# Second-layer scan of a two-layer hybrid trunk: TensorE's order fixed to the program's, with the fp32 matmuls and transposes of a chunk in one block

## The chip, the core and the metric

The kernel runs on one core of one Trainium2 chip. The metric is the device time of one execution in microseconds, the median of several runs. A profile of one execution shows where its time goes; the engines are named as on its page: PE is TensorE (matmuls and transposes), PEld its weight loads, DVE VectorE, ACT ScalarE, POOL GpSimd, SP the queue from which all transfers are issued.

## What is computed

Two layers over 1024 tokens of width 1024: a gated DeltaNet layer and a Mamba-2 layer, each with a residual add, then a final RMSNorm. The change concerns the second layer alone:

```python
proj = hid @ w_in                                   # 1024 x 6176
z, xbc, dt = split(proj)                            # 2048, 4096, 32
xbc = silu(causal_conv(xbc, conv_w) + conv_b)
xs, Bm, Cm = split(xbc)                             # 32 heads x 64; 8 groups x 128, twice
# chunks of 128 tokens, 8 groups of 4 heads
cb     = C_chunk @ B_chunk.T                        # per group
y_diag = (cb * exp(acs_l - acs_s), lower) @ X       # per head
states = B.T @ (decay * X);  S = S * dec + states   # per group, chunk after chunk
y_off  = C @ S_before * exp(acs)
y = rmsnorm_per_group((y_diag + y_off + D * xs) * silu(z))
out = x + y @ w_out
```

## The kernel before

**Tiling.** Tokens stand in eight chunks of 128. The normalised input of a layer is kept transposed as `hid`, split into a high and a low part, and every projection is three matmuls of parts (L165 to L167, L227 to L229), so that the product has nearly fp32 precision. The scan's own products are plain fp32 matmuls, and 128 x 128 transposes are matmuls against an identity (L66).

**Second layer.** A loop over the eight head groups (L949 to L959; it starts at -1 to produce the first group's inputs) runs two generators side by side for eight slots. `J` makes the next group's inputs: each slot is one projection half, 24 matmuls of 512 columns into one bank `ps_proj` (`proj_halves`), whose result is copied, convolved by three operations on DVE (L204) and passed through SiLU. For the half of the channels that are X, four transposes (`ps_pt<-ident,acc`) are put into a list, `later`, and are issued behind the next half's matmuls or by `flush()`. `S` is the scan of the present group (`scan`), one chunk per slot:

- `store(n-1)` transposes the normalised result `yn` of the chunk before (two L66 transposes into `ps_tr`), scales it and sends it to DRAM for the output projection;
- `prep(n+1)` makes B·C for the next chunk (L856) and B transposed (L66, `ps_tr<-ident,BC`), the decay matrix `lt` by four exponentials on ACT (L866) from the rows `gcrow`, and their product `mt` on DVE (L868). The rows come by four transfers for every four chunks (L316) and are masked by four operations on POOL (L317);
- `z_chunk` is the gate z for the chunk: 24 matmuls of 256 columns into `ps_proj`;
- `main(n)` is the state update (L882), C·S (L892) and the diagonal products: 16 matmuls of 64 columns (L895, L896), each into one half of the partitions. Their sum goes through five operations on DVE, a square with a sum on ACT (L906), two small operations on POOL (L907, L909) and a scaling on DVE (L910), which gives `yn`.

The last group has no J; it computes two z chunks per slot in its first four slots, and the output projection (L347 to L349) follows.

**What sets the order.** The kernel is written in this program order, but the order in which an engine gets its instructions is chosen by the scheduler, from the dependencies, the program's order as priority and a model of the engines' times. Each engine then takes its instructions in the order given.

Of the kernel before, what the change touches and what calls it, by code (L numbers as in the profile page):

```python
# [1 line left out]

# [17 lines left out]
NT = T // P  # L20
# [4 lines left out]
def hybrid_trunk(  # L25
# [194 lines left out]
    def z_chunk(pool, hid, zw, n, z=None):  # L220
        zh, zl = zw
        pt = ps_proj()[:, 0:256]
        th, o = n // 4, (n % 4) * P
        for k in range(KT):
            xh = hid["h", k // 4, th][:, k % 4, o:o + P]
            xl = hid["l", k // 4, th][:, k % 4, o:o + P]
            nc.tensor.matmul(pt, xh, zh[:, k, :], start=k == 0, stop=False)  # L227
            nc.tensor.matmul(pt, xh, zl[:, k, :], start=False, stop=False)  # L228
            nc.tensor.matmul(pt, xl, zh[:, k, :], start=False, stop=k == KT - 1)  # L229
        tz = pool.tile([P, 256], F32, tag="tz", name="tz", bufs=1)  # L230
        if z is None:
            z = pool.tile([P, 256], F32, tag="z", name="z", bufs=2)
        nc.scalar.activation(tz, pt, AF.Tanh, scale=0.5)
        nc.vector.scalar_tensor_tensor(out=z, in0=tz, scalar=1.0, in1=pt, op0=ALU.add, op1=ALU.mult)  # L234
        return z
# [167 lines left out]
    with tc.tile_pool(name="gw", bufs=2) as gw:  # L403
# [360 lines left out]
        for g in range(8):  # L764
            J = todo["K"] if g == 0 else js_of(g)
# [37 lines left out]
    with tc.tile_pool(name="sw", bufs=2) as sw:  # L803
# [39 lines left out]
        def scan(g):  # L843
# [5 lines left out]
            def prep(n):  # L849
                if n % 4 == 0:  # L850
                    for h in range(4):
                        rows[h] = gc_rows(sw, "gcrow", Gs["gcr"], h0 + h, n // 4, 4)
                c = slice(n * P, (n + 1) * P)
                BT, CT, xn_ = BC[:, 0, c], BC[:, 1, c], xs[:, n, :]
                pt = ps_tr()
                nc.tensor.matmul(pt[:, 0:P], BT, CT, start=True, stop=True)  # L856
                btok = xw = None
                if n < NT - 1:
                    turn_pe(pt[:, P:2 * P], BT, ident)
                    xw = sw.tile([P, 256], F32, tag="xw", name="xw")  # L860
                    nc.gpsimd.tensor_tensor(out=v4(xw), in0=v4(xn_), in1=bc4(dtd, n), op=ALU.mult)
                    btok = sw.tile([P, P], F32, tag="bt", name="bt")
                    nc.scalar.activation(btok, pt[:, P:2 * P], AF.Copy, scale=0.5)
                lt = sw.tile([P, 4, P], F32, tag="L", name="lt")
                for h in range(4):
                    nc.scalar.activation(lt[:, h, :], rows[h][:, n % 4, :], AF.Exp, bias=ldt[:, h0 + h, n:n + 1])  # L866
                mts = sw.tile([P, 4, P], F32, tag="M", name="mt")
                nc.vector.tensor_tensor(out=mts, in0=pt[:, 0:P].unsqueeze(1).broadcast_to([P, 4, P]), in1=lt,  # L868
                                        op=ALU.mult)
                t2 = sw.tile([P, 256], F32, tag="t2", name="t2")  # L870
                nc.gpsimd.tensor_tensor(out=v4(t2), in0=v4(xn_),
                                        in1=dskip[:, h0:h0 + 4].unsqueeze(2).broadcast_to([P, 4, 64]), op=ALU.mult)
                A[n] = btok, xw, mts, t2
# [40 lines left out]
            def store(n):  # L914
                yn = Y.pop(n)
                pt = ps_tr()
                yg = sw.tile([P, 2, P], F32, tag="yg", name="yg")
                for i in range(2):
                    turn_pe(pt[:, i * P:(i + 1) * P], yn[:, i * P:(i + 1) * P], ident)
                for i in range(2):  # L920
                    nc.scalar.activation(yg[:, i, :], pt[:, i * P:(i + 1) * P], AF.Copy,
                                         scale=snw[:, 2 * g + i:2 * g + i + 1])
                nc.sync.dma_start(yd1[n][g * 256:(g + 1) * 256, :].rearrange("(h p) t -> p h t", p=P), yg)
# [4 lines left out]
            if g == 7:  # L928
                zt = bpool.tile([P, NT, 256], F32, tag="a0", name="z7", bufs=2)
            for n in range(NT):  # L930
                if n > 0:
                    store(n - 1)
                if n < NT - 1:
                    prep(n + 1)
                if g < 7:
                    Z[n] = z_chunk(sw, hid2, zw, n)
                elif n < 4:
                    for m in (2 * n, 2 * n + 1):
                        Z[m] = z_chunk(sw, hid2, zw, m, zt[:, m, :])
                S = main(n, S, Z.pop(n))  # L940
                yield
            store(NT - 1)

# [5 lines left out]
        for g in range(-1, 8):  # L949
            its = [bc_halves(g + 1) if g >= 0 else bc0, x_halves(g + 1)] if g < 7 else []  # L950
            J = (y_ for it in its for y_ in it)
            S = scan(g) if g >= 0 else iter(())
            for slot in range(8):
                next(S, None)
                next(J, None)
            flush()
            next(S, None)
            if g < 7:
                GS[g + 1]["zw"] = load_zw(bpool, sw_in, (g + 1) * 256, ("a2", "a3"), 2)  # L959

# [33 lines left out]
```

## Time and profile before

| | us |
|---|---|
| median of 3 runs | 1995.43 (1994.64 to 2000.03) |
| the profiled execution's own time | 1990.66 |
| its span on the chip | 1989.0 |
| PE busy | 1919.1 (96%) |
| DVE busy | 1305.7 (66%) |
| ACT busy | 1063.4 (53%) |
| POOL busy | 411.6 (21%) |

The span runs from the first to the last instruction; 1.66 us of the execution's time lie around it. Busy PE is not PE at its peak: matmuls overlap, so the time that one costs is the distance from its start to the start of the next. In a timeline row, x2 joins two neighbouring instructions (each fp32 product of L856, L882 and L892 shows as two), and a bracket at its end names an idle stretch before the row and what ended it.

### The profile page before, as it was taken

The page shows a single profiled execution, that of the slowest core. Times are in us where ns is not written, and L with a number is a line of the kernel's source. Part 1 is how long each engine was busy: PE and PEld are TensorE (multiplying, and loading weights), DVE is VectorE, ACT ScalarE, POOL GpSimd, SP SyncE. Part 2 cuts the span into 40 slices and gives each one's busy share as a digit, 9 for nine tenths or more (in the row PEclk, how much of TensorE's full clock was granted, in tenths as well). Part 3 has the DMA queues.
Part 4 walks back from the last instruction along what each step waited for, and adds up shares of the span by engine and source line. Part 5 has one row for each costly group of instructions (what it writes and reads, how often), then busy time and mean ns, then how long its engine had stood idle before and what let it go on. Part 6 is the DMA issues. An engine that isn't in the chain of part 4 may idle for free.

```text
span 1989.0 us, 36043 instructions
## 1 busy us (share of the span) xinstructions
PE 1919.1 (96%) x12974; PEld 1639.7 (82%) x12974; DVE 1305.7 (66%) x2915; ACT 1063.4 (53%) x2893; POOL 411.6 (21%) x818
## 2 busy tenths in 40 slices
PE   7997999999999999999999999999999999999998
PEld 5786888888888888897778788888888888888886
DVE  6797685778677776844354676657666676767333
ACT  5635656575656666564343554544555555555332
POOL 1101211212122212100000032423333243332000
PEclk9997999999999999999999999999999999999999
DMA  4421323232232323235574232222222223236654
GB/s 141 117 54 49 98 56 84 67 78 75 57 93 52 99 49 105 58 94 157 152 221 133 64 91 80 69 84 80 64 80 57 80 75 83 78 104 195 203 170 142
DMA packets 284789, 193.35 MB, mean 97 GB/s; under 512 B 65425, under 2 KB 246338, under 8 KB 284610
## 3 DMA queue, kind: packets, MB, share of 16 engines
q1 hardware_dynamic: 284610, 191.05, 34.2%
q8 instruction: 102, 1.67, 0.4%
q14 instruction: 77, 0.63, 0.1%
HBM read 159.34 MB, written 31.65 MB: 96 GB/s over the span
## 4 chain that ended last, share of the span: by engine, by line
PE 75%; DMA 9%; DVE 7%; ACT 4%; POOL 2%; issue 2%; SPq 1%; POOLq 0%; DVEq 0%; ACTq 0%
PE ps_proj L165 9%; PE ps_proj L166 9%; PE ps_proj L167 9%; PE ps_proj L347 6%; PE ps_proj L349 6%; PE ps_proj L348 5%; PE ps_proj L227 5%; PE ps_proj L228 4%; PE ps_proj L229 4%; DMA gcrow<-gcr_s 2%; PE ps_tr L66 2%; PE ps_pt L66 2%; DMA X<-xd 2%; DVE acc L204 2%; PE ps_sc L895 1%
## 5 line engine op out<-in xcount | busy, mean ns | idle before, releaser
L165 PE MATMUL ps_proj<-hid_h,wh 128*128 128x512 f32 x1024 | 412.9, 403 | 3.4 <-ACT acc L200 3.2
L167 PE MATMUL ps_proj<-hid_h,wl 128*128 128x512 f32 x1024 | 404.9, 395 | 0.0
L166 PE MATMUL ps_proj<-hid_l,wh 128*128 128x512 f32 x1024 | 403.6, 394 | 0.0
L227 PE MATMUL ps_proj<-zh,hid_h 128*128 128x256 f32 x1024 | 300.5, 293 | 1.0 <-DVE z L234 1.0
L229 PE MATMUL ps_proj<-zh,hid_l 128*128 128x256 f32 x1024 | 295.4, 288 | 0.0
L228 PE MATMUL ps_proj<-zl,hid_h 128*128 128x256 f32 x1024 | 295.4, 288 | 0.0
L165 PEld LDWEIGHTS ps_proj<-hid_h,wh 128*128 128x128 f32 x1024 | 192.7, 188 | 43.9 <-ACT acc L200 4.0
L167 PEld LDWEIGHTS ps_proj<-hid_h,wl 128*128 128x128 f32 x1024 | 192.5, 188 | 40.3
L166 PEld LDWEIGHTS ps_proj<-hid_l,wh 128*128 128x128 f32 x1024 | 192.9, 188 | 35.4
L347 PE MATMUL ps_proj<-woh,yh 128*128 128x512 f32 x512 | 205.2, 402 | 4.6 <-ACT yh L86 3.2
L348 PE MATMUL ps_proj<-wol,yh 128*128 128x512 f32 x512 | 204.4, 400 | 0.8 <-DVE wol L87 0.7
L349 PE MATMUL ps_proj<-woh,yl 128*128 128x512 f32 x512 | 203.1, 399 | 0.8 <-DVE yl L87 0.7
L227 PEld LDWEIGHTS ps_proj<-zh,hid_h 128*128 128x128 f32 x1024 | 196.3, 192 | 6.0 <-DVE z L234 2.3
L228 PEld LDWEIGHTS ps_proj<-zl,hid_h 128*128 128x128 f32 x1024 | 196.4, 192 | 3.0
L229 PEld LDWEIGHTS ps_proj<-zh,hid_l 128*128 128x128 f32 x1024 | 196.4, 192 | 0.3
L204 DVE SCALAR_TENSOR_TENSOR acc<-raw,cw_ssd,acc 128x512 f32<-128x512 f32 x192 | 156.5, 815 | 45.2 <-ACT acc L202 42.5
L86 ACT CAST yh<-yr 128x512 fp32r<-128x512 f32 x128 | 79.1, 619 | 142.2 <-PE ps_proj L348 90.8
L87 DVE TENSOR_TENSOR yl<-yr,yh 128x512 fp32r<-128x512 f32 x128 | 89.0, 696 | 98.7 <-ACT yh L86 98.3
L204 DVE SCALAR_TENSOR_TENSOR acc<-raw,cw_gdn,acc 128x512 f32<-128x512 f32 x192 | 145.9, 761 | 11.8 <-ACT acc L200 10.2
L87 DVE TENSOR_TENSOR wl<-wr,wh 128x512 fp32r<-128x512 f32 x128 | 89.3, 698 | 68.3 <-ACT wh L86 67.7
L317 POOL TENSOR_SCALAR_AFFINE_SELECT gcrow<-gcrow 128x512 f32<-128x512 f32 x128 | 92.1, 722 | 197.1 <-DMA gcrow<-gcr_g 141.8
L676 POOL TENSOR_SCALAR so<-so,cq 128x2 f32<-128x2 f32 x64 | 27.3, 426 | 462.7 <-ACT yn L675 462.7
(240 smaller groups left out, 3872.0 us busy)
## 6 DMA issues: line engine op xcount, KB each, us to landing
wr<-in_gdn_w_in_dram SPq DMA_DIRECT2D x96, 256.0 KB, 3.0
wr<-in_ssd_w_in_dram SPq DMA_DIRECT2D x96, 256.0 KB, 2.9
gcrow<-gcr_g SPq DMA_DIRECT2D x64, 256.0 KB, 3.6
yr<-y0d SPq DMA_DIRECT2D x64, 256.0 KB, 3.4
gcrow<-gcr_s SPq DMA_DIRECT2D x64, 256.0 KB, 3.9
yr<-y1d SPq DMA_DIRECT2D x64, 256.0 KB, 3.2
y0d<-yg SPq DMA_DIRECT2D x64, 128.0 KB, 1.9
wr<-in_gdn_w_out_dram SPq DMA_DIRECT2D x32, 256.0 KB, 3.5
```

What stands on the lines that cost most here:

```text
L87: nc.vector.tensor_tensor(out=lo, in0=src, in1=hi.bitcast(F32), op=ALU.subtract)
L165: nc.tensor.matmul(pt[0:nco], hi[:, j, 0:nco], xh[:, j, :], start=first, stop=False)
L166: nc.tensor.matmul(pt[0:nco], hi[:, j, 0:nco], xl[:, j, :], start=False, stop=False)
L167: nc.tensor.matmul(pt[0:nco], lo[:, j, 0:nco], xh[:, j, :], start=False, stop=last)
L204: nc.vector.scalar_tensor_tensor(out=acc, in0=raw[:, k:k + 512], scalar=cw[:, k * 32 + ti:k * 32 + ti + 1], in1=acc, op0=ALU.mult, op1=ALU ...
L227: nc.tensor.matmul(pt, xh, zh[:, k, :], start=k == 0, stop=False)
L228: nc.tensor.matmul(pt, xh, zl[:, k, :], start=False, stop=False)
L229: nc.tensor.matmul(pt, xl, zh[:, k, :], start=False, stop=k == KT - 1)
L317: nc.gpsimd.affine_select(out=t, in_=t, pattern=[[0, 4], [1, P]], compare_op=ALU.is_ge, fill=-1e30, base=0, channel_multiplier=-1)
L347: nc.tensor.matmul(pt, yh[:, j, :], hi[:, j, :], start=first, stop=False)
L348: nc.tensor.matmul(pt, yh[:, j, :], lo[:, j, :], start=False, stop=False)
L349: nc.tensor.matmul(pt, yl[:, j, :], hi[:, j, :], start=False, stop=last)
```

## The change

In `scan` the order within a slot becomes z, prep(n+1), main(n), store(n-1). In the loop the slot's projection half now comes ahead of the scan's chunk. For groups 0 to 6 the whole is put under a manual schedule of PE: inside it, PE gets its instructions in the program's order and the scheduler orders the other engines alone. Group -1 and group 7, and everything outside the second layer's loop, remain with the scheduler.

```diff
-            for n in range(NT):
-                if n > 0:
-                    store(n - 1)
-                if n < NT - 1:
-                    prep(n + 1)
                 if g < 7:
                     Z[n] = z_chunk(sw, hid2, zw, n)
                 elif n < 4:
                     for m in (2 * n, 2 * n + 1):
                         Z[m] = z_chunk(sw, hid2, zw, m, zt[:, m, :])
+                if n < NT - 1:
+                    prep(n + 1)
                 S = main(n, S, Z.pop(n))
+                if n > 0:
+                    store(n - 1)
                 yield
...
-            for slot in range(8):
+            order = tc.manual_schedule(engines={mybir.EngineType.PE}) if 0 <= g < 7 else nullcontext()
+            with order:
+                for slot in range(8):
+                    next(J, None)
+                    next(S, None)
+                flush()
                 next(S, None)
-                next(J, None)
-            flush()
-            next(S, None)
```

On PE, in group 0, chunk 5, the diagonal products (L895, L896) stood in two pieces before, with the transposes of the chunk before and the next chunk's B·C between them; L882 of this chunk stood ahead of the z matmuls:

```order
L229 MATMUL ps_proj<-zh,hid_l_11585 128x256
L892 MATMUL ps_sc<-S,BC 128x256
L895 MATMUL ps_sc<-xs,mt 64x64
L896 MATMUL ps_sc<-xs,mt 64x64
L66 MATMUL ps_tr<-ident,yn 128x128 x2
L856 MATMUL ps_tr<-BC 128x128
L66 MATMUL ps_tr<-ident,BC 128x128
L895 MATMUL ps_sc<-xs,mt 64x64
L896 MATMUL ps_sc<-xs,mt 64x64
```

In the changed kernel the same place reads as follows, and so does nearly every chunk of groups 0 to 6:

```order
L229 MATMUL ps_proj<-zh,hid_l_11585 128x256
L856 MATMUL ps_tr<-BC 128x128
L66 MATMUL ps_tr<-ident,BC 128x128
L882 MATMUL ps_sc<-xw,bt 128x256
L892 MATMUL ps_sc<-S,BC 128x256
L895 MATMUL ps_sc<-xs,mt 64x64
L896 MATMUL ps_sc<-xs,mt 64x64
L895 MATMUL ps_sc<-xs,mt 64x64
L896 MATMUL ps_sc<-xs,mt 64x64
L895 MATMUL ps_sc<-xs,mt 64x64
L896 MATMUL ps_sc<-xs,mt 64x64
L895 MATMUL ps_sc<-xs,mt 64x64
```

One L896 row more closes these 16 matmuls (a row stands for two), then come the two `yn` transposes and the next projection half (L165). Over the whole second layer the order of before holds 83 unbroken pieces of L895 and L896 for 64 chunks; the changed one holds 64.

On POOL, late in a group, the four maskings of the next rows stood ahead of the two operations (L907, L909) that lead to `yn`:

```order
L871 TENSOR_TENSOR t_15385<-xs,dskip 128x256
L317 AFFINE_SELECT gcrow<-gcrow 128x512 x4
L907 TENSOR_SCALAR so<-so 128x1
L909 TENSOR_TENSOR so<-so,expo 128x1
L196 COPY raw<-raw 128x3
```

Now two of the maskings come behind them:

```order
L871 TENSOR_TENSOR t_15454<-xs,dskip 128x256
L317 AFFINE_SELECT gcrow<-gcrow 128x512
L907 TENSOR_SCALAR so<-so 128x1
L317 AFFINE_SELECT gcrow<-gcrow 128x512
L909 TENSOR_TENSOR so<-so,expo 128x1
L317 AFFINE_SELECT gcrow<-gcrow 128x512 x2
L887 TENSOR_TENSOR S<-S,egl_s 128x256
```

The first slot of a group on PE, in the changed kernel, where two of the fixed blocks meet: the last transposes and the last store of the group before stand behind the new group's first projection half, and `prep` of its first chunk has only the 24 z matmuls between it and its use.

```order
L167 MATMUL ps_proj<-hid_h_11580,wl 128x512
L66 MATMUL ps_pt<-ident,acc 128x128 x4
L66 MATMUL ps_tr<-ident,yn 128x128 x2
L856 MATMUL ps_tr<-BC 128x128
L66 MATMUL ps_tr<-ident,BC 128x128
L227 MATMUL ps_proj<-zh,hid_h_11578 128x256
```

Behind these rows follow the other z matmuls, L856 of the second chunk, and L882 and L895 of the first.

## Rows read from the trace of the kernel before

**Rows 1.** The page, parts 1 and 2: busy time, and TensorE's granted clock in 40 slices.

```profile
PE 1919.1 (96%) x12974; PEld 1639.7 (82%) x12974; DVE 1305.7 (66%) x2915; ACT 1063.4 (53%) x2893; POOL 411.6 (21%) x818
PEclk9997999999999999999999999999999999999999
```

**Rows 2.** Windows: length, then busy PE, PEld, DVE, ACT, POOL (instructions), clock, DMA share, GB/s.

```profile
1155.00:1766.40 611.40, 606.62 (x4201) 522.39 (x4201) 403.71 (x739) 321.36 (x847) 202.98 (x375) 1.00 0.26 74
1766.40:1840.00 73.60, 73.25 (x513) 62.08 (x513) 53.59 (x105) 42.69 (x110) 21.48 (x39) 1.00 0.61 187
```

**Rows 3.** Waits of PE from 1155 to 1840: us in total, times, longest.

```profile
PE ps_tr L66 <- DVE yn L910: 4.3, 7, 1.5
PE ps_pt L66 <- DVE acc L185: 0.7, 1, 0.7
```

**Rows 4.** Timeline of PE: transposes and B·C between z matmuls (start, length, what).

```profile
1200.82 0.28 PE L227 MATMUL ps_proj<-zh,hid_h 128*128 128x256 f32 x1
1200.94 0.38 PE L66 MATMUL ps_tr<-ident,yn 128*128 128x128 f32 x2
1201.16 0.39 PE L856 MATMUL ps_tr<-BC 128*128 128x128 f32 x2
1201.38 0.27 PE L66 MATMUL ps_tr<-ident,BC 128*128 128x128 f32 x1
1201.41 0.36 PE L228 MATMUL ps_proj<-zl,hid_h 128*128 128x256 f32 x1
1201.61 0.28 PE L229 MATMUL ps_proj<-zh,hid_l 128*128 128x256 f32 x1
```

**Rows 5.** Timeline of PE: a chunk whose diagonal products are in one piece.

```profile
1202.87 0.59 PE L892 MATMUL ps_sc<-S,BC 128*128 128x256 f32 x2
1203.40 0.27 PE L895 MATMUL ps_sc<-xs,mt 128*64 128x64 f32 x1
...
1204.01 0.50 PE L165 MATMUL ps_proj<-hid_h,wh 128*128 128x512 f32 x1
1204.35 0.39 PE L166 MATMUL ps_proj<-hid_l,wh 128*128 128x512 f32 x1
1204.58 0.40 PE L167 MATMUL ps_proj<-hid_h,wl 128*128 128x512 f32 x1
```

**Rows 6.** Timeline of PE: a chunk whose diagonal products are in two pieces.

```profile
1256.85 0.59 PE L892 MATMUL ps_sc<-S,BC 128*128 128x256 f32 x2
...
1257.75 0.44 PE L66 MATMUL ps_tr<-ident,yn 128*128 128x128 f32 x2
1258.02 0.39 PE L856 MATMUL ps_tr<-BC 128*128 128x128 f32 x2
...
1259.28 0.40 PE L166 MATMUL ps_proj<-hid_l,wh 128*128 128x512 f32 x1
```

**Rows 7.** Timelines of POOL, DVE and PE: the longest wait for `yn`.

```profile
1299.57 1.08 POOL L317 TENSOR_SCALAR_AFFINE_SELECT gcrow<-gcrow 128x512 f32<-128x512 f32 x1 [2.17 <-DMA gcrow<-gcr_s]
1301.48 0.35 DVE L910 TENSOR_SCALAR yn<-y,so 128x256 f32<-128x256 f32 x1 [0.99 <-POOL so L909]
1301.89 0.44 PE L66 MATMUL ps_tr<-ident,yn 128*128 128x128 f32 x2 [1.51 <-DVE yn L910]
```

**Rows 8.** Tile `gcrow`, 1195 to 1325: transfers from issue to landing.

```profile
DMA to landing us min/median/max: 3.2/3.9/6.5
```

**Rows 9.** Timeline of DVE: from diagonal products to `yn`, undisturbed chunk.

```profile
1280.26 0.42 DVE L898 TENSOR_TENSOR y<-ps_sc,t 128x256 f32<-128x256 f32 x1
1284.40 0.34 DVE L910 TENSOR_SCALAR yn<-y,so 128x256 f32<-128x256 f32 x1
```

**Rows 10.** Windows: a block of fp32 work, then a fall of the clock in layer 1.

```profile
1256.42:1258.94 2.52, 2.52 (x27) 1.83 (x26) 2.45 (x4) 0.38 (x1) 2.43 (x5) 1.00 0.00 0
365.00:372.00 7.00, 3.84 (x18) 2.59 (x17) 3.47 (x19) 4.51 (x17) 1.97 (x6) 1.00 0.37 77
372.00:375.60 3.60, 3.60 (x19) 3.54 (x19) 3.50 (x14) 1.50 (x5) 0.00 (x0) 0.53 0.13 36
```

More of the change, by code (lines that the diff above doesn't have):

```diff
@@ L1 @@
-from contextlib import ExitStack
+from contextlib import ExitStack, nullcontext
 import concourse.bass as bass
```

## The prediction, written before the changed kernel ran

> **What bounds the kernel now.** I read the page first: PE is busy for 96% of the span at the full granted clock in nearly every slice [rows 1]. So PE sets the time, and the question for a change of order is what PE loses between useful matmuls. The windows give the stretch that the change rewrites: from the first L856 of group 0 to the start of group 7 (1155 to 1766.4) PE is busy for 606.62 of 611.40 us, and in group 7 up to the last scan transposes for 73.25 of 73.60 [rows 2]. True idle time is thus about 5.1 us, and the waits of PE name 5.0 of it: seven waits for `yn`, 4.3 us together, and one of 0.7 us for the transposes of X [rows 3]. A wait for weights, for z or for a `ps_proj` bank is not in that list. The rest of what an order can win must lie inside the busy time, as spacing that is wider than the matmuls need, and only the timeline shows that.
>
> **What an order costs inside busy time.** I take each distance from start to start.
>
> *z matmuls against fp32 work.* z matmuls follow one another every 0.12 us. In [rows 4] the row at 1200.82 and the one at 1201.61 are two z steps apart, 0.24 us undisturbed, and are 0.79 us apart; so the two `yn` transposes, B·C and the B transpose cost 0.55 us there. Their own spacing is 0.22 + 0.22 us for two transposes and for B·C, and half of 0.22 for the one B transpose: 0.55. Going from the split-precision matmuls to fp32 ones and back costs nothing that can be read. What the description of the change is mostly about, fewer passages between projection work and fp32 work, is therefore worth 0.
>
> *Diagonal products.* These matmuls of 64 columns are another matter. In one piece: from L892 at 1202.87 to the second projection matmul at 1204.35 it is 1.48 us [rows 5]. In two pieces: from L892 at 1256.85 to the second projection matmul at 1259.28 it is 2.43 us [rows 6], of which 0.55 us are the transposes and B·C in between, by their price above. So a split costs 2.43 − 1.48 − 0.55 = **0.40 us**. The order has 83 pieces for 64 chunks before and 64 pieces now, 19 fewer: 19 × 0.40 = **7.6 us**. (14 of the 19 lie in groups 0 to 6, two per group; five in group 7, which the new written order also puts right though the scheduler still has it.)
>
> *What follows the products.* When a projection comes next, its first matmul takes 0.34 us instead of 0.23 [rows 5]: 0.11 lost. When the `yn` transposes come next, they take 0.27 us instead of 0.22 [rows 4, 6]: 0.05 lost. The change puts the transposes there in all 56 chunks of groups 0 to 6 (the projection behind them then starts from an ordinary transpose, which is free as shown): 56 × 0.06 = **3.4 us**.
>
> *Waits.* The `yn` transposes move behind main(n). Counted from L892 they come after the whole block, 0.6 us later than in a split, and `prep` (0.33 us) now also stands ahead of L892; so `yn` is asked for about 0.7 us later (the rest of the block included). Undisturbed, `yn` is ready 4.5 us after the products (1280.26 to 1284.74 [rows 9]), and the next slot asks for it after a projection half (24 × 0.23 = 5.5 us), z (24 × 0.12 = 2.9 us) and the block: ample. In the longest case it was late because the maskings of `gcrow` stood ahead of it on POOL, waiting for transfers [rows 7], and there POOL now has only two of the four ahead of L909. The single 0.7 us wait goes as well, since a projection half of 5.5 us now stands ahead of it. All **5.0 us** of waits should go.
>
> Upper sum: 7.6 + 3.4 + 5.0 = 16.0 us.
>
> **What the change adds.** No instruction is added, and nothing crosses a queue except by order: on SP the stores of `yn` go out some 2 us later, with the weight and row loads behind them in about the same sequence as before. The new danger is that PE cannot step aside any more: what is late at its place holds all projections behind it. I looked for the tightest places. (a) First slot of a group: `mt` of chunk 0 needs L856, then DVE, and is asked for once z (2.9 us), transposes, B·C and L882 are through, under 4 us later; before that DVE must take convolution steps of the projection half that has just ended. (b) The last z-weight part and the rows: ACT casts or exponentiates them in its own order, and where they are late the copy that frees the projection's bank is late behind them. That copy has the time of z and the block, some 5 us; a transfer of 3.9 us fits in it, one of 6.5 us does not [rows 8]. Neither place shows a wait of PE now, so the trace has no row for its price. Below it is 0; above, I take the longest wait seen, 1.51 us [rows 7], twice per group: 14 × 1.5 = 21 us. I take 2 us, close to the lower end, because both places have room for the median case and seven waits for a similar cause come to 4.3 us today.
>
> Sum: 16.0 − 2.0 = **14.0 us**. The profiled execution of 1990.66 us (span 1989.0) would become 1976.7. The median of the runs shown is 4.8 us above that execution, and I carry that over: **1981.4 us**. A difference of 0.3%, 6 us, is about what a measurement of this kernel tells from no change.
>
> **Rivals.**
>
> *Waits stay, in other places.* The waits of 5.0 us remain in their size (POOL still has maskings ahead of L907 and L909), and fixed order adds as much again in the first slots. Gain 16.0 − 10.0 = 6 us: 1989.4. For it: POOL, ACT and DVE orders were rebuilt around the new PE order, and seven waits exist today. Against: `yn` is asked for later. Chance 0.18, half of it on either side of 6 us.
>
> *Slower: the rows hold everything.* Rows of `gcrow` land late, ACT stands at its exponentials, the copy out of `ps_proj` behind them is late, and PE, in fixed order, stands at the next projection, where the scheduler before could place other work. It decides once it costs more than the 16.0 us won: with 14 loads, 1.15 us each makes it even, and 1.6 us each (22 us) makes it 6 us slower, 2001.8 us. For it: landing times up to 6.5 us and the 2.17 us that POOL waited for one [rows 7, 8]. Against: 1.51 us is the longest wait seen today [rows 7], and all 14 would have to pass it. Chance 0.06.
>
> *Slower: the clock falls.* In layer 1 the granted clock fell to half (0.53 over 3.6 us, level 1.2 GHz) behind a stretch in which PE was busy for 3.84 of 7.00 us [rows 10]. If the new block did the same once per chunk, each fall would cost (1 − 0.53) × 3.6 = 1.7 us; 56 of them are 95 us, and with the 14 won the time is 2076. Twelve falls would be enough for slower. Against: 2.52 us of just such work, products, transposes and B·C, ran at 1.00, with PE never idle [rows 10], and the new block holds the same kinds of work in about that time. Chance 0.02. The Trainium skill ("TensorE: Matmul & The Clock Gate", Part 4, PE-mode transpose) says that transposes do not count as activity for the clock in the way matmuls do; by that rule gathering them into one block speaks against this change. The trace does not agree that a block of this size suffices.
>
> That the order is not what the change says can be excluded for groups 0 to 6: PE's order shows the block in each chunk, with 24 projection and 24 z matmuls between.
>
> **How the numbers follow.** Forecast 0.74, waits stay 0.18, rows 0.06, clock 0.02. Faster by over 0.3%: 0.74 + 0.09 = 0.83; within: 0.09; slower: 0.08. The low end takes no new waits, 16.0 us, an error of 0.02 us in each of the 19 + 56 places, 1.5 us, and 3 us for the runs' own spread: 1975. The high end, 1992, takes in most of the first rival; what lies beyond is the two slower ones and its tail. The forecast's own range is 1977 to 1987.
>
> **What would show it.** Right: unbroken runs of 16 diagonal matmuls in the timeline, 0.27 us for the transposes behind them, the first projection matmul at 0.23; no wait of PE for `yn`; the stretch from the first L856 to the last scan transposes about 14 us shorter; everything ahead of it as before; the clock at 9 in every slice of layer 2. Wrong: PE waiting for `mt`, for `ps_proj` (released by ACT or DVE) or for `yn` in its list of waits for more than 6 us in total; or a split that turns out to cost less than 0.4 us, seen as a slot that is not shorter though its products are in one piece.

## The result, and the profile after

The changed kernel takes **1981.41 us** (median, 1977.69 to 1984.13) where the kernel before takes 1995.43 us (1991.1 to 2003.13) in the same comparison: a ratio of 0.9923, 95% interval 0.9903 to 0.9943. That is 14.0 us by the medians, and anything from 11 to 19 us by the interval. The forecast was 1981.4 us. How much of this is the sum being right, and how much luck, the trace has to tell.

The page of the changed kernel, parts 1 and 2, answers to [rows 1]:

```profile
span 1979.9 us, 36018 instructions
PE 1909.3 (96%) x12974; PEld 1633.9 (83%) x12974; DVE 1312.4 (66%) x2915; ACT 1067.0 (54%) x2893; POOL 412.6 (21%) x818
PEclk9997999999999999999999999999999999999999
```

PE's busy time fell by 9.8 us with the same 12974 instructions, and the clock digits are the same in all 40 slices.

The layers have to be told apart, since the first one is not touched by the change. Its end can be read at one row of PE's timeline, the last transposes of `gtmp`, and the end of the second layer at the last output matmul. Changed kernel:

```profile
1147.58 0.38 PE L66 MATMUL ps_tr<-ident,gtmp 128*128 128x128 f32 x2
...
1972.46 0.40 PE L349 MATMUL ps_proj<-woh,yl 128*128 128x512 f32 x1
```

Kernel before:

```profile
1144.95 0.38 PE L66 MATMUL ps_tr<-ident,gtmp 128*128 128x128 f32 x2
...
1981.55 0.40 PE L349 MATMUL ps_proj<-woh,yl 128*128 128x512 f32 x1
```

From row to row the second layer took 836.60 us before and 824.88 us now: **11.7 us less**. The first layer came out 2.6 us longer in this one profile, without any change of its order; over the profiles of this study the first row stands between 1144.7 and 1153.5 us. This stretch of the second layer is therefore the better measure: a second profile of the changed kernel gave 824.90. Of the kernel before there is one profile.

A chunk of the changed kernel, timeline of PE, answers to [rows 5, 6]:

```profile
1262.96 0.59 PE L892 MATMUL ps_sc<-S,BC 128*128 128x256 f32 x2
1263.48 0.27 PE L895 MATMUL ps_sc<-xs,mt 128*64 128x64 f32 x1
...
1264.10 0.44 PE L66 MATMUL ps_tr<-ident,yn 128*128 128x128 f32 x2
1264.29 0.48 PE L165 MATMUL ps_proj<-hid_h,wh 128*128 128x512 f32 x1
1264.61 0.40 PE L166 MATMUL ps_proj<-hid_l,wh 128*128 128x512 f32 x1
1264.84 0.39 PE L167 MATMUL ps_proj<-hid_h,wl 128*128 128x512 f32 x1
```

All 16 diagonal products take 0.62 us to the transposes, these 0.19 us to the projection, and its first matmul 0.32 us.

The waits of PE from 1150 us to the end answer to [rows 3] (the columns are the same):

```profile
PE ps_proj L347 <- ACT yh L86: 1.1, 1, 1.1
PE ps_tr L66 <- DVE yn L910: 0.8, 1, 0.8
PE ps_pt L66 <- DVE acc L185: 0.3, 1, 0.3
PE ps_sc L895 <- DVE mt L868: 0.3, 1, 0.3
PE ps_proj L347 <- ACT woh L86: 0.3, 1, 0.3
```

Only the two rows of 0.3 us, for `acc` and for `mt`, lie in groups 0 to 6, both in the first slots of group 0; the wait for `yn` that is left lies in group 7, and L347 is the output projection. Windows of PE, changed kernel, the first from inside group 0 to the end of group 6 (columns as in [rows 2]):

```profile
1163.00:1757.00 594.00, 593.38 (x4189) 514.57 (x4189) 409.04 (x738) 321.53 (x835) 204.47 (x374) 1.00 0.27 76
1757.00:1840.00 83.00, 80.53 (x541) 67.19 (x540) 57.66 (x110) 47.61 (x124) 22.13 (x40) 1.00 0.64 200
```

In 594 us PE is idle for 0.6 us. All of the new idle time stands in the second window, 2.5 us.

Why `yn` is no longer late: in groups 0 to 6 all waits of PE for it but one were for the `yn` of a group's chunk 4 (chunks count from 0), the case of [rows 7]. Here is that chunk in group 1. Kernel before, PE's first diagonal product, then ACT up to the square L906 (between them and the transposes stand the rows of [rows 7]):

```profile
1290.04 0.27 PE L895 MATMUL ps_sc<-xs,mt 128*64 128x64 f32 x1
...
1298.81 0.62 ACT L86 CAST zh<-wr 128x512 fp32r<-128x512 f32 x1 [5.75 <-DMA wr<-in_ssd_w_in_dram]
1299.34 0.41 ACT L906 ACTIVATE yn<-y 128x256 f32<-128x256 f32 x1
```

Changed kernel, PE, ACT, POOL, DVE and PE again:

```profile
1294.90 0.27 PE L895 MATMUL ps_sc<-xs,mt 128*64 128x64 f32 x1
...
1299.03 0.41 ACT L906 ACTIVATE yn<-y 128x256 f32<-128x256 f32 x1
...
1301.15 0.64 POOL L317 TENSOR_SCALAR_AFFINE_SELECT gcrow<-gcrow 128x512 f32<-128x512 f32 x1 [3.50 <-DMA gcrow<-gcr_s]
...
1303.08 0.71 DVE L910 TENSOR_SCALAR yn<-y,so 128x256 f32<-128x256 f32 x1 [3.23 <-POOL so L909]
...
1306.44 0.44 PE L66 MATMUL ps_tr<-ident,yn 128*128 128x128 f32 x2
```

Before, `yn` was written 11.8 us behind the chunk's first product, and PE had stood for it since 10.3. Now it is written after 8.9 us and asked for after 11.5: 2.65 us to spare. Two orders changed ahead of it. On ACT, L906 stood behind a cast that waited for z weights and came to its end, with its read-out, after 9.8 us; now it is through after 4.6. On POOL, two of the four maskings now come behind L909. The prediction had named POOL alone. All seven groups show the same: L906 through after 8.3 to 9.8 us before and 4.6 to 5.3 now, `yn` after 10.3 to 11.8 and 8.5 to 10.4. The least that was to spare in groups 0 to 6 was 1.1 us.

### The profile page after: what moved, and what is told of

Read it like the earlier page. It is cut to its first block, busy times and chain, and to the rows that moved or that the text cites. A ratio compares the mean times of both kernels' runs of the same rounds, so it can differ in the third digit from the quotient of the medians.

```text
span 1979.9 us, 36018 instructions
## 1 busy us (share of the span) xinstructions
PE 1909.3 (96%) x12974; PEld 1633.9 (83%) x12974; DVE 1312.4 (66%) x2915; ACT 1067.0 (54%) x2893; POOL 412.6 (21%) x818
## 4 chain that ended last, share of the span: by engine, by line
PE 75%; DMA 9%; DVE 7%; ACT 3%; issue 2%; POOL 2%; SPq 1%; POOLq 0%; DVEq 0%; ACTq 0%
PE ps_proj L165 9%; PE ps_proj L166 9%; PE ps_proj L167 9%; PE ps_proj L227 5%; PE ps_proj L229 5%; PE ps_proj L228 5%; PE ps_proj L347 5%; PE ps_proj L349 5%; PE ps_proj L348 5%; PE ps_tr L66 2%; DMA X<-xd 2%; PE ps_pt L66 2%; PE ps_sc L895 2%; DVE acc L204 1%; PE ps_sc L634 1%
## 5 line engine op out<-in xcount | busy, mean ns | idle before, releaser
L165 PE MATMUL ps_proj<-hid_h,wh 128*128 128x512 f32 x1024 | 411.7, 402 | 3.1 <-ACT acc L200 2.7
L165 PEld LDWEIGHTS ps_proj<-hid_h,wh 128*128 128x128 f32 x1024 | 192.7, 188 | 41.0 <-ACT acc L200 3.5
L347 PE MATMUL ps_proj<-woh,yh 128*128 128x512 f32 x512 | 205.5, 402 | 9.2 <-ACT yh L86 6.6
L204 DVE SCALAR_TENSOR_TENSOR acc<-raw,cw_gdn,acc 128x512 f32<-128x512 f32 x192 | 146.1, 762 | 12.5 <-ACT acc L200 10.9
L86 ACT CAST wh<-wr 128x512 fp32r<-128x512 f32 x128 | 79.1, 620 | 99.0 <-PE ps_proj L166 89.1
```

What stands on the lines that cost most here:

```text
L86: nc.scalar.copy(hi, src)
L165: nc.tensor.matmul(pt[0:nco], hi[:, j, 0:nco], xh[:, j, :], start=first, stop=False)
L204: nc.vector.scalar_tensor_tensor(out=acc, in0=raw[:, k:k + 512], scalar=cw[:, k * 32 + ti:k * 32 + ti + 1], in1=acc, op0=ALU.mult, op1=ALU ...
L347: nc.tensor.matmul(pt, yh[:, j, :], hi[:, j, :], start=first, stop=False)
```

## The experiments

Two measures are used beside the ratio. The *stretch* is the second layer's length from row to row as above. The *loss* is a distance on PE less the spacing that its instructions need when undisturbed (0.227 us for a matmul of 512 columns, 0.118 for z, 0.109 for a transpose and for each half of B·C, 0.215 for each half of L882 and L892, 0.031 for a diagonal product); it is taken in three parts: groups 0 to 6 (first L856 to the last diagonal product of group 6), group 7 (from there to its last diagonal product; some output matmuls stand in it too) and the output matmuls behind. The instructions are the same in all kernels, so differences of loss are differences of time. In brackets is the part of it that is idle time. A *piece* is an unbroken run of L895 and L896.

| kernel | pieces | ratio to before (95%) | stretch, us | loss in groups 0 to 6 | loss in group 7 | loss behind |
|---|---|---|---|---|---|---|
| before | 83 | 1 | 836.6 | 31.6 (4.8) | 5.2 (0.4) | 2.8 (0.0) |
| changed | 64 | 0.9923 (0.9903 to 0.9943) | 824.9 | 18.2 (0.6) | 4.2 (1.1) | 5.4 (1.4) |
| the same again, `f4_again` | 64 | 0.9920 (0.9899 to 0.9941) | 824.9 | 18.3 (0.7) | 2.8 (0.0) | 6.7 (1.6) |
| `e1_split` | 114 | 1.0002 (0.9987 to 1.0018) | 842.4 | 35.8 (0.7) | 3.2 (0.0) | 6.4 (2.5) |
| `e2_store_first` | 64 | 0.9939 (0.9922 to 0.9957) | 826.3 | 20.7 (0.7) | 3.5 (0.4) | 5.0 (1.5) |
| `e3_z_cut` | 64 | 0.9948 (0.9930 to 0.9966) | 825.8 | 19.4 (0.7) | 3.3 (0.2) | 6.1 (1.6) |
| `e4_order_only` | 64 | 0.9918 (0.9897 to 0.9940) | 822.7 | 17.9 (0.4) | 2.8 (0.0) | 5.0 (1.0) |
| `e5_fix_only` | 66 | 1.0409 (1.0379 to 1.0439) | 918.1 | 111.0 (58.6) | 5.0 (0.5) | 5.1 (1.9) |
| `e6_g7` | 64 | 0.9972 (0.9954 to 0.9991) | 833.9 | 18.3 (0.7) | 11.6 (5.4) | 7.0 (1.8) |
| `f2_j_first` | 79 | 0.9969 (0.9957 to 0.9981) | 832.4 | 25.6 (0.5) | 4.7 (1.2) | 5.0 (1.4) |
| `f3_scan_first` | 65 | 0.9931 (0.9908 to 0.9953) | 825.4 | 19.8 (1.8) | 2.9 (0.0) | 5.7 (1.7) |
| `e7_pairs` | 41 | 0.9914 (0.9889 to 0.9939) | 819.3 | 14.6 (2.6) | 3.7 (1.5) | 4.0 (0.4) |
| `f1_pairs_free` | 41 | 0.9908 (0.9891 to 0.9926) | 819.9 | 13.8 (1.6) | 3.4 (1.2) | 5.7 (1.8) |
| `e8_pairs_g7` | 40 | 0.9966 (0.9953 to 0.9978) | 829.7 | 13.8 (1.7) | 10.7 (6.6) | 8.2 (2.9) |

The theory at the start: the gain is that the diagonal products are no longer split, that transposes follow them, and that `yn` is not waited for. Rival A: it is the fewer passages between projection or z matmuls and fp32 work (315 in the second layer before, 213 now). Rival B: it is the fixing of PE's order itself.

### What one split costs: `e1_split`

The changed kernel, with the store put back into the middle of the products:

```diff
                 for ha, hb in ((0, 1), (1, 0), (2, 3), (3, 2)):
+                    if ha == 2 and n > 0:
+                        store(n - 1)
...
                 S = main(n, S, Z.pop(n))
-                if n > 0:
-                    store(n - 1)
                 yield
```

> The changed kernel, with store(n-1), two yn transposes, put between the second and the third pair of diagonal products in every chunk but a group's first, so that they stand in two pieces again: 114 pieces instead of 64; passages between split-precision and fp32 work as in the changed kernel (213). Theory (a piece of diagonal products has a price of its own, 0.40 us per split, and another 0.06 us where a projection instead of yn transposes follows): 50 x 0.40 + 49 x 0.06 = 23 us slower than the changed kernel, about 2004 us, with no new wait of PE. Rival (what was gained is the smaller number of passages between projection work and fp32 work, 315 before and 213 now): no difference, 1981 us.

Measured 1998.03 us where before takes 1996.53: the whole gain is gone, with the waits as rare as in the changed kernel. Timeline of PE, one chunk:

```profile
1267.96 0.27 PE L897 MATMUL ps_sc<-xs,mt 128*64 128x64 f32 x1
...
1268.35 0.44 PE L66 MATMUL ps_tr<-ident,yn 128*128 128x128 f32 x2
1268.71 0.27 PE L897 MATMUL ps_sc<-xs,mt 128*64 128x64 f32 x1
...
1269.10 0.50 PE L165 MATMUL ps_proj<-hid_h,wh 128*128 128x512 f32 x1
1269.43 0.40 PE L166 MATMUL ps_proj<-hid_l,wh 128*128 128x512 f32 x1
```

From the first product to the second projection matmul it is 1.47 us, against 1.13 us in the chunk of the changed kernel above, for the same instructions. Eight products take 0.39 us where sixteen take 0.62, and the transposes between two pieces 0.36 instead of 0.19. Over groups 0 to 6 the loss grew by 17.6 us for 49 more pieces: **0.36 us** each, in which is the worse exit that the next run prices. The expectation of 23 us was too large: it took the 0.40 us of a split that also has B·C and the transpose of B in it.

### What follows the products: `e2_store_first`

```diff
-                S = main(n, S, Z.pop(n))
                 if n > 0:
                     store(n - 1)
+                S = main(n, S, Z.pop(n))
```

> The changed kernel with store(n-1) ahead of main(n) instead of behind it: the fp32 work stays one block and the products one piece (64), but a projection follows them in 55 places instead of 7. Theory: 48 x 0.06 = 2.9 us slower; yn is asked for 1.6 us earlier, and since its smallest slack in groups 0 to 6 of the changed kernel is 1.1 us, at most 1 us of waits; about 1985 us. Rival (passages alone count, 217 against 213): no difference.

The products stay whole, and the projection follows them. Loss in groups 0 to 6: 20.7 instead of 18.2, 2.5 us in 48 chunks: **0.05 us** each. (This is read from the profiles; the ratios of the two kernels don't tell them apart.) So a split by itself is 0.36 − 0.05 = 0.31 us in `e1_split`.

### Passages alone: `e3_z_cut`

The changed kernel, with `prep` issued in the middle of the z matmuls, so that two more passages stand in each slot (309 instead of 213) and everything else stays:

```diff
         for k in range(KT):
+            if k == 4 and mid is not None:
+                mid()
...
-                    Z[n] = z_chunk(sw, hid2, zw, n)
+                    Z[n] = z_chunk(sw, hid2, zw, n, mid=(lambda: prep(n + 1)) if n < NT - 1 else None)
...
-                if n < NT - 1:
+                if g == 7 and n < NT - 1:
                     prep(n + 1)
```

> The changed kernel with prep(n+1), B x C and the B transpose, in the middle of the 24 z matmuls: fp32 work of a chunk in two blocks, 309 passages instead of 213, pieces of products 64 as before. Theory (passages are free): the same time within 2 us, 1981 us. Rival (the 11.7 us that the second layer won between the two profiles belong to 102 fewer passages, 0.115 us each): 96 x 0.115 = 11 us slower, 1992 us.

Timeline of PE at the cut:

```profile
1265.19 0.28 PE L231 MATMUL ps_proj<-zh,hid_l 128*128 128x256 f32 x1
1265.31 0.38 PE L858 MATMUL ps_tr<-BC 128*128 128x128 f32 x2
1265.53 0.27 PE L66 MATMUL ps_tr<-ident,BC 128*128 128x128 f32 x1
1265.56 0.37 PE L229 MATMUL ps_proj<-zh,hid_h 128*128 128x256 f32 x1
1265.76 0.28 PE L230 MATMUL ps_proj<-zl,hid_h 128*128 128x256 f32 x1
```

From L858 to L230 it is 0.45 us, for B·C, one transpose and one z matmul, which need 3 × 0.109 + 0.118 = 0.445. Over groups 0 to 6, 96 more passages cost 1.2 us, 0.012 us each. Rival A, which wanted some 11 us, is refuted. (The median differs from the changed kernel's by more than that; in the profile the first layer was 4.2 us longer, and the stretch only 0.9.)

### The order without the fixing, and the fixing without the order: `e4_order_only`, `e5_fix_only`

`e4_order_only` keeps the new written order and takes the manual schedule away:

```diff
-            order = tc.manual_schedule(engines={mybir.EngineType.PE}) if 0 <= g < 7 else nullcontext()
+            order = nullcontext()
```

> The new written order alone, with the scheduler ordering PE as before (no manual schedule). It reaches 64 pieces of diagonal products by itself, with the yn transposes behind 50 of them, but 239 passages between projection or z matmuls and fp32 work instead of 213. Theory (pieces and what follows them set the gain): within 2 us of the changed kernel, so 1981 to 1984. Rival (the fixed order, and the passages it saves, bring it): 26 passages more at 0.11 us, 3 us, plus any waits that the fixing removed; 1985 or above, and if fixing were all of it, the time of before, 1995.

1976.66 us beside 1993.11, ratio 0.9918: the same as with the fixing. The scheduler makes nearly the same order by itself, with 64 pieces, and its waits of PE in the second layer are two:

```profile
PE ps_proj L347 <- ACT yh L86: 0.8, 1, 0.8
PE ps_pt L66 <- DVE acc L185: 0.4, 1, 0.4
```

`e5_fix_only` is the changed kernel with the written order of before, under the manual schedule:

```diff
             for n in range(NT):
+                if n > 0:
+                    store(n - 1)
+                if n < NT - 1:
+                    prep(n + 1)
...
-                if n < NT - 1:
-                    prep(n + 1)
                 S = main(n, S, Z.pop(n))
-                if n > 0:
-                    store(n - 1)
...
-                    next(J, None)
                     next(S, None)
+                    next(J, None)
                 flush()
```

> The written order of before under the manual schedule of PE in groups 0 to 6: 66 pieces, every one in these groups followed by a projection, yn transposes right behind the projection half and ahead of z. Theory: 17 pieces fewer save 5 to 7 us, but yn is asked for about 1.9 us earlier in the slot than the scheduler had it, and PE cannot pass it: waits for yn appear in the slots where it was already thin (slots 0 and 4 of a group had 0.06 us to spare), 14 of them at 1.5 to 3.5 us, 20 to 50 us; so slower than before, about 2010. Rival (passages count, 271 instead of 315, and no new waits): 5 to 7 us for the pieces and 44 at 0.1 for the passages, about 1985 to 1988.

2073.08 us, ratio 1.0409. The direction was right, the size not: 58 us of waits where 20 to 50 were expected, and a second loss that was not expected at all. The waits of PE:

```profile
PE ps_pt L66 <- DVE acc L185: 34.6, 7, 5.6
PE ps_tr L66 <- DVE yn L910: 21.6, 8, 4.0
```

The waits for `yn` were foreseen. The 5.6 us for `acc` were not: at the end of a group `flush()` follows the last projection half at once, and its transposes need three convolution steps and a SiLU of that very half. Timelines of PE and DVE there:

```profile
1248.96 0.39 PE L167 MATMUL ps_proj<-hid_h,wl 128*128 128x512 f32 x1
...
1254.53 0.84 DVE L185 SCALAR_TENSOR_TENSOR acc<-th,acc 128x512 f32<-128x512 f32 x1 [0.76 <-ACT th L184]
...
1255.43 1.11 PE L66 MATMUL ps_pt<-ident,acc 128*128 128x128 f32 x4 [5.64 <-DVE acc L185]
```

In the changed kernel the scan's chunk stands between the two, since the projection half comes first in the slot. Behind such a wait the clock falls. Windows of `e5_fix_only`:

```profile
1249.00:1254.50 5.50, 0.79 (x6) 0.46 (x4) 3.42 (x4) 2.90 (x5) 2.99 (x4) 1.00 0.35 92
1254.50:1261.30 6.80, 5.74 (x25) 5.34 (x26) 2.23 (x3) 3.95 (x13) 0.32 (x1) 0.50 0.07 19
1261.30:1310.00 48.70, 48.70 (x340) 41.49 (x339) 30.22 (x57) 21.82 (x59) 17.39 (x33) 1.00 0.26 76
1163.00:1757.00 594.00, 540.40 (x3552) 463.52 (x3552) 345.27 (x632) 272.21 (x716) 169.46 (x319) 0.95 0.23 65
```

PE is busy for 0.79 of 5.50 us, then runs at 1.2 GHz (0.50) for 6.8 us, then at full speed again. Over the 594 us the mean is 0.95, that is some 30 us lost. It agrees with the loss: it grew by 79.4 us, 53.8 of it idle; the other 25.6, with 14 pieces fewer in these groups (5.6 us won at 0.40), leave 31.2 for the clock. In sum the waits thus cost about 1.6 times their length here, though not each of them: behind one of 2.6 us, at 1809.2 us, the clock stayed at 1.00.

So rival B is refuted in both directions: fixing alone makes the kernel 4% slower, and the order alone has the whole gain.

### Which part of the order: `f2_j_first`, `f3_scan_first`

Both are the kernel before with one of the two edits to the written order. `f2_j_first`:

```diff
-                next(S, None)
                 next(J, None)
+                next(S, None)
             flush()
```

> The kernel before with one part of the new written order: the projection half ahead of the scan's chunk in a slot, the scan itself and the scheduler as before. 79 pieces instead of 83, 55 of them followed by a projection. Theory: 4 pieces fewer at 0.35 us, 1.4 us, and the waits for yn about as they were; between 4 us below and 2 us above the kernel before, ratio 0.998 to 1.001. Rival (this part carries the gain, since it moves yn back): ratio 0.995 or below.

`f3_scan_first` changes the scan alone (z, `prep`, `main`, `store`):

```diff
             for n in range(NT):
-                if n > 0:
-                    store(n - 1)
-                if n < NT - 1:
-                    prep(n + 1)
...
+                if n < NT - 1:
+                    prep(n + 1)
                 S = main(n, S, Z.pop(n))
+                if n > 0:
+                    store(n - 1)
                 yield
```

> The kernel before with the other part alone: z, prep, main, store inside the scan, the projection half behind it as before, the scheduler as before. 65 pieces, 51 of them followed by the yn transposes. Theory: this part carries the whole gain, 12 to 16 us, ratio 0.992 to 0.994. Rival (the store is asked for earlier without the projection half ahead of the chunk, so the waits for yn stay): 5 us less, 0.9945 to 0.996.

`f2_j_first` missed its band, ratio 0.9969 for 0.998 to 1.001, and its rival's (0.995 or below) too: the theory had left the waits where they were, but its idle time in groups 0 to 6 fell from 4.8 to 0.5 us. No wait for `yn` is left there; the only one in its profile is in group 7. `f3_scan_first` fell as expected, 0.9931. It takes the pieces from 83 to 65, and the loss in groups 0 to 6 without idle time from 26.8 to 18.0 us, against 17.6 in the changed kernel; of the idle time it leaves 1.8 us. So the scan's order gives the spacing, some 8.9 of 9.2 us, and either edit takes most of the waits.

### Group 7, and two chunks' products in one piece: `e6_g7`, `e7_pairs`, `e8_pairs_g7`, `f1_pairs_free`

`e6_g7` fixes PE's order in group 7 too:

```diff
-            order = tc.manual_schedule(engines={mybir.EngineType.PE}) if 0 <= g < 7 else nullcontext()
+            order = tc.manual_schedule(engines={mybir.EngineType.PE}) if 0 <= g else nullcontext()
```

> The changed kernel with the manual schedule in group 7 as well: yn transposes behind 52 pieces instead of 50. Theory: group 7 already has one piece per chunk, so nothing to win there: within 2 us of the changed kernel, 1980 to 1983, and the waits in the output projection behind it (2 to 3 us, for its weights and the last yh) stay. Rival (those waits come from the scheduler's order in group 7): 2 to 3 us less, and no waits of PE after 1790 us.

It is 9 us longer than the changed kernel by the stretch; neither theory had this. Timeline of PE where group 6 ends:

```profile
1750.38 0.44 PE L66 MATMUL ps_tr<-ident,yn 128*128 128x128 f32 x2
1753.85 1.11 PE L66 MATMUL ps_pt<-ident,acc 128*128 128x128 f32 x4 [3.03 <-DVE acc L185]
1757.35 0.69 PE L66 MATMUL ps_tr<-ident,yn 128*128 128x128 f32 x2 [2.38 <-DVE yn L910]
```

No projection half follows here, and with group 7 fixed as well nothing may pass the flush; in the changed kernel the scheduler has 39 z matmuls of group 7 at this place. The clock fell to 0.50 from 1753.0 to 1763.2 us. The waits in the output projection stayed, so they don't come from the order in group 7.

`e7_pairs` makes the products of two chunks in one piece (chunks 1 and 2, 3 and 4, 5 and 6; 0 and 7 alone), with one sum on DVE for both. The core of it:

```diff
+            pairs = {0: [0], 1: [1, 2], 3: [3, 4], 5: [5, 6], 7: [7]}
...
-                for ha, hb in ((0, 1), (1, 0), (2, 3), (3, 2)):
-                    nc.tensor.matmul(py[64:128, hc[hb]], mts[:, hb, 64:128], xn_[:, hc[hb]], start=True, stop=True)
-                    nc.tensor.matmul(py[0:64, hc[ha]], mts[:, ha, 0:64], xn_[:, hc[ha]], start=True, stop=True)
...
+                if n in pairs:
+                    w = 256 * len(pairs[n])
+                    py = ps_sc()
+                    for i, m in enumerate(pairs[n]):
+                        pm, mts, xm = py[:, i * 256:(i + 1) * 256], A[m][2], xs[:, m, :]
+                        for ha, hb in ((0, 1), (1, 0), (2, 3), (3, 2)):
+                            nc.tensor.matmul(pm[64:128, hc[hb]], mts[:, hb, 64:128], xm[:, hc[hb]], start=True, stop=True)
+                            nc.tensor.matmul(pm[0:64, hc[ha]], mts[:, ha, 0:64], xm[:, hc[ha]], start=True, stop=True)
...
-                if n < NT - 1:
-                    prep(n + 1)
+                if n == 0:
+                    prep(1)
+                elif n < NT - 2:
+                    prep(n + 2)
                 S = main(n, S, Z.pop(n))
+                if n == 0:
+                    prep(2)
```

> The changed kernel with the diagonal products of chunks 1 and 2, 3 and 4, 5 and 6 of a group in one piece of 32 matmuls (prep runs two chunks ahead, C x S and the state update have banks of their own, and one VectorE operation adds the skip term of both chunks): 41 pieces instead of 64, passages 207. Theory (a piece costs some 0.30 us beyond its matmuls): 23 x 0.30 = 7 us faster than the changed kernel, 1974 us, if no wait is added. Rival (passages): 6 fewer, under 1 us.

1977.30 us, ratio 0.9914. The stretch is 5.5 us shorter than the changed kernel's, where 7 us were expected without new waits; in groups 0 to 6 the loss without idle time fell by 5.6 us for 21 pieces fewer, 0.27 us each, and 2.0 of it went back into waits. `f1_pairs_free` is the same without the manual schedule (`order = nullcontext()`), `e8_pairs_g7` with group 7 fixed as well.

> The paired version (diagonal products of two chunks in one piece) without the manual schedule. It has 41 pieces by the scheduler's own order too, but 235 passages instead of 207. Theory (pieces and what follows them, not the fixing): within 2 us of the paired version with PE fixed, so 17 to 21 us below the kernel before, ratio 0.990 to 0.9915. Rival (the fixing is what keeps PE from standing): idle time of PE in the second layer rises above the 4.5 us of the fixed one, 0.993 or above.

> The version with the diagonal products of two chunks in one piece (41 pieces), with the manual schedule in group 7 too. Theory: the order in group 7 is worth nothing by itself, so within 2 us of the paired version, 1975 to 1979. Rival: PE stands in group 7, which has no projection halves between its chunks, for the pair's mt and y, and what the pairs won there is lost: 1980 or above.

`f1_pairs_free` measures 0.9908, as the theory had it: 1977.71 us beside 1995.98, with a stretch 5.0 us shorter than the changed kernel's. It or `e7_pairs`, which can't be told apart, is the best version of this study: by their stretches ahead of both kernels, though by the ratios' intervals not proven faster than the changed one. `e8_pairs_g7` missed its theory and loses behind group 6 what `e6_g7` lost, by the rival's count if not for its reason: PE waits there for the last `acc` and for `yn`.

### The changed kernel again: `f4_again`

> The changed kernel itself once more, beside the three parts, to have its ratio and the spread of a second profile on the same chip. Theory: ratio 0.992 to 0.994 as first measured, equal to the new written order without the fixing (0.9918 to within 0.002); the stretch from the end of the first layer to the last matmul of the output projection within 2 us of the first profile's. Rival (the fixing costs or gives something that a second look shows): over 4 us away from the version without it.

0.9920 for 0.9923, and 824.90 us for 824.88. The version without the fixing has a stretch 2.2 us shorter, of which 1.9 lie behind group 6, where waits differ from profile to profile (2.5 and 1.6 us idle in the two of the changed kernel). The fixing is worth nothing here that these runs can tell.

## Why the prediction was right

By its steps, in the second layer's stretch: 14.0 us forecast, 11.7 measured. That the medians differ by just 14.0 is luck: they lie within the spread of this, and are no proof of the sum.

- **Passages worth nothing: right.** 0.012 us each, 1.2 us for the 102 that the change saves. The forecast took 0.
- **Split, 0.40 us: right, and the largest term.** It was read from one chunk, and holds for all: from the first product to the second projection matmul the kernel before loses 0.63 us, idle time left out, in each of the 14 chunks of groups 0 to 6 with two pieces (mean; 0.60 to 0.71) and 0.23 in the 42 with one. In these groups the loss without idle time fell by 9.2 us, and the terms as measured make 14 × 0.40 + 49 × 0.05 + 1.2, some 9.3. With only the transposes between the pieces a split costs 0.31 (`e1_split` less `e2_store_first`); why it is 0.40 with B·C and the transpose of B there too, no run tried.
- **Five splits in group 7, 2.0 us: right in group 7, but lost behind it.** From 13 pieces to 8, the loss without idle time fell there from 4.9 to 3.2 us (2.8 in `f4_again`). The output projection behind, which the steps left out, lost 2.6 us more than before (3.9 in `f4_again`).
- **Exit, 0.06 × 56 = 3.4 us: a little large.** It is 0.05, and holds in 49 chunks: in a group's first slot a projection still follows. 2.5 us. The loss also stands at another row than forecast: the transposes take 0.19 and the first projection matmul 0.32, 0.51 together, where 0.27 and 0.23 were named.
- **Waits, 5.0 us: right in groups 0 to 6, by a reason that was read in part.** The idle time fell there from 4.8 to 0.6 us. PE asks for the `yn` of chunk 4 1.2 us later than before, where 0.7 was forecast. That `yn` itself comes sooner, by 0.1 to 2.9 us, was put down to POOL's maskings alone; of the longest case these held L907 for 0.8 us only (from 1299.85, the end of L906, to 1300.63), and ahead of that L906 had been late on ACT. Each edit to the written order by itself has the `yn` of chunk 4 in time: `f2_j_first` asks after 10.0 us and has it after 8.3 to 9.9, `f3_scan_first` asks after 11.1 and has it after 9.5 to 10.9.
- **New waits, 2.0 us: right in size, wrong in place.** The danger was seen at `mt` in a group's first slot, which cost 0.3 us once in the whole layer, and at the rows of `gcrow`, which cost nothing: their transfers took at most 4.9 us to land in the same part of the program, 6.5 before [rows 8]. The idle time came behind group 6 instead, 2.1 us more than before: 0.7 in group 7 and 1.4 in the output projection. ACT and PE timelines of the changed kernel:

```profile
1831.04 0.62 ACT L86 CAST woh<-wr 128x512 fp32r<-128x512 f32 x1 [1.93 <-DMA wr<-in_ssd_w_out_dram]
1832.46 0.62 ACT L86 CAST woh<-wr 128x512 fp32r<-128x512 f32 x1 [0.80 <-DMA wr<-in_ssd_w_out_dram]
1832.98 0.61 ACT L86 CAST yh<-yr 128x512 fp32r<-128x512 f32 x1
...
1833.65 0.50 PE L347 MATMUL ps_proj<-woh,yh 128*128 128x512 f32 x1 [1.12 <-ACT yh L86]
```

ACT stands for the output weights' transfers, casts `yh` behind them, and PE waits for that. This is read from the rows alone; no run tried to bring those transfers forward.

In sum, groups 0 to 6 gave 13.4 us where the steps had 12.0 for them, group 7 gave 1.0 where they had 2.0, and the output projection, for which they had nothing, took 2.6.

Of the rivals, the waits that stay and the rows of `gcrow` are refuted by the 0.6 us of idle time in groups 0 to 6. The clock fell nowhere in the changed kernel's second layer ahead of the last output matmul (1.00 in the windows above). Its block of products and transposes ran at full speed, as the prediction's row of 2.52 us had suggested [rows 10]; where the clock did fall (`e5_fix_only`, `e6_g7`, `e8_pairs_g7`), PE had stood idle just ahead of it, in one wait of 2.1 us or more or in two shorter ones close together. Not every such wait was followed by a fall: 2.3 us in `e1_split` and 2.6 us in `e5_fix_only` were not. The Trainium skill ("TensorE: Matmul & The Clock Gate", Part 1, What's actually happening) has an idle TensorE fall back to half its rate; the 0.50 behind the waits agrees with that. For the rule on transposes in the same page of the Trainium skill (Part 4, PE-mode transpose), no run here shows a cost.

## What to carry to other kernels

When one engine is busy for 96%, look for the time inside its busy rows: take distances from start to start around each kind of neighbour, and price a switch by one chunk that has it and one that has not. Write the program so that each group of small products stays whole and its result is asked for well after it is ready; here the scheduler then found the order, and a fixed order added nothing. Where an order is fixed, check every place at which a result is used right behind the work that makes it, the ends of loops above all: here one such place per group cost 5.6 us of waiting and a slow clock behind it. And look at what stands behind the changed part: an output projection that comes sooner can wait for its inputs, and it took back 2.6 us here.

## What was not expected of the hardware

- A piece of 64-column products costs about 0.3 us beyond its products, whether it holds 8, 16 or 32 (0.31 by `e1_split`, 0.27 by `e7_pairs`; 0.40 in the splits of the kernel before), while going from split-precision matmuls to fp32 ones and transposes costs 0.012 us. The products write 64 of 128 partitions, the other matmuls all of them (128*64 and 128*128 in the rows). The Trainium skill ("TensorEngine Tiling (Array Packing)", Key Properties) says that a change of the tiling mode drains TensorE; the dearer entry and exit of a piece agree with it, but no run here changed the tiling mode alone.
- The waits of `e5_fix_only`, most of them 2.6 to 5.6 us long, cost more than half as much again, by a clock that went to 1.2 GHz behind 13 stretches of waiting (6.8 us of it in the windows shown); the single wait of 1.5 us in [rows 7] left it at full speed.
